# Hybrid Hyena and attention layer on one core: thirteen gate pairs by seven half-products, placed behind all branch projections

## The chip, the cores and the metric

The kernel runs on one core of a Trainium2 chip. The time is device microseconds for one launch; the span is the time from the first to the last instruction in the hardware profile of one such execution. Lower is better.

## The reference

One encoder layer: 512 tokens, width 2048, all in float32. Cut to what matters here:

```python
h = rms_norm(x, mix_norm_g)                       # (512, 2048)
proj = h @ w_in
u_h, q, k, v, g = jnp.split(proj, [c0, c1, c2, c3], axis=-1)   # g: 2 x 2048 columns
y_h = ...        # Hyena branch, (512, 1024), from u_h
y_a = ...        # attention branch, (512, 1024), from q, k, v
g_h, g_a = jnp.split(jax.nn.sigmoid(g + b_gate), 2, axis=-1)
merged = g_h * (y_h @ w_br_hyena) + g_a * (y_a @ w_br_attn)
x = x + merged @ w_out
h2 = rms_norm(x, ffn_norm_g)
return x + (jax.nn.silu(h2 @ w_ffn_gate) * (h2 @ w_ffn_up)) @ w_ffn_down   # inner width 5632
```

The merge, on which the change works, is the line of `merged` with the 2 x 2048 gate columns of `proj`: 16 blocks of 128 channels, and for each block one gate column block for Hyena, one for attention, and one branch projection of each.

## The kernel before

Activations lie with channels on the 128 partitions and the 512 tokens along the free axis. A matrix product takes 128 x 128 weight blocks as the stationary operand and a 128 x 512 activation tile as the moving one. For float32 accuracy each operand is split into a rounded high part and a remainder (`hi`, `lo`), and a block costs three matmuls (`mm3`): hi x hi, hi x lo, lo x hi.

Weights are packed by the host into tiles of eight blocks (512 KB) in the order of use (`weight_blocks`). `wblk` loads the next tile on SP's queue into one of two `raw` buffers, ScalarE casts the high part (three buffers), VectorE subtracts to get the remainder (three buffers). `group` runs one output block over its k blocks. `tmp` is a pool of five 128 x 512 scratch tiles that all stages share. PSUM has eight banks.

Instructions are written with tiles and the framework's scheduler orders them within each engine's queue; only TensorE's are kept in the order in which they are written. A queue runs in the order that the scheduler chose, and waits are on semaphores. The pools marked `reuse_waits="tile"` lie over older ones and wait tile by tile.

Stages, in TensorE's order:

1. Hyena projections, filters and convolutions; attention. Their results are `yh` and `ya`, eight tiles each, in pool `r3`. The normalised input `xg` stays split in pool `r1` (16 `hi`, 16 `lo`).
2. Merge. `gate_pair(m)` computes the two gate blocks of channel block m: two groups of 16 k blocks, 96 matmuls, then on VectorE a multiplication by the token scale `rbc` and on ScalarE a sigmoid. Three pairs (`GATES_AHEAD`) run ahead. Then, for each m, two branch groups of eight k blocks (48 matmuls), a multiplication of each by its gate, an addition into the merged row `mg`, and the gate pair m + 3. The branch inputs are split into a pool `r2` of their own.
3. The 16 merged rows, all in SBUF, are split into `r1` (`ms`), and 16 groups make the output projection `o`. `x2_tile` adds the residual, `x_sums` and `x_split` prepare what the FFN needs.
4. FFN gate and up. Two k halves, two columns blocks and two token halves make a 2 x 2 block product, done with seven products of halves in place of eight. `x_sums` builds the seven combinations of the activation for a pair of rows p (tile `V`, 128 x 7 x 256), `x_split` splits them (tile `X`; five pairs live in pool `xa`, three in `xb`, which lies over `r1`). For each group, VectorE builds four sums of weight tiles (`wsum`), ScalarE and VectorE split seven weight tiles (`wsplit`), `product` runs eight matmuls of 512 columns and eight of 256 for each of the seven, over PSUM banks `x` (two), `y` and `z`, and `fold` and half-width VectorE steps add the results up. The first group is written apart, since pairs 5 to 7 can be split only when `r1` is free, and takes in the norm of the new rows (`rs2`). 44 groups; `finish` closes each.
5. Down projection in three parts, most activations by way of DRAM (`actd`, `actr`), with the first four outputs side by side (`WIDE`).

The seven products, as the groups run them (`hl` is a split weight tile, `i` the combination of activations):

```python
for p in range(p0, p1):
    x = xs[p][:, i * 2 * H:(i + 1) * 2 * H]
    mm(bank, hi[:, p * P:(p + 1) * P], x, first and p == 0, False, skip_group_check=True)
for p in range(p0, p1):
    x = xs[p][:, i * 2 * H:(i * 2 + 1) * H]
    mm(bank[:, H:], lo[:, p * P:(p + 1) * P], x, False, p == NP - 1, skip_group_check=True)
```

Of the kernel before, what the change touches and what calls it, by code (L numbers as in the profile page):

```python
# [56 lines left out]
def weight_blocks():  # L57
# [25 lines left out]
    def quadrant(name, half, j):  # L83
        return [(name, k * P, j * P, P) for k in range(half, KT, 2)]

    for j in range(0, FT, 2):
        for name in ("w_ffn_gate", "w_ffn_up"):
            for half, c in ((0, 0), (0, 1), (1, 1), (1, 0)):
                out += quadrant(name, half, j + c)
# [11 lines left out]
def layer_kernel(tc, wpk, xT, par, flt, zemb, w4, decT, tbl, tb2, rope, qkg, out):  # L101
# [10 lines left out]

    def ps_tile(name):
        return psm.tile([P, S], F32, tag="ps", bufs=8, name=name)
# [622 lines left out]

    gts = [gate_pair(m) for m in range(GATES_AHEAD)]
# [3 lines left out]
    r2 = tc.alloc_tile_pool(name="r2", bufs=1)  # L742
    yhs = [split(r2, t, "hi2", "lo2", 16, 16, f"yhs{i}") for i, t in enumerate(yh)]
    yas = [split(r2, t, "hi2", "lo2", 16, 16, f"yas{i}") for i, t in enumerate(ya)]

    merged = []
    for m in range(KT):
        gs = gts[m]
        mg = r3.tile([P, S], F32, tag="r", bufs=16, name=f"mg{m}")
        for i, src in enumerate((yhs, yas)):  # L750
            bp = ps_tile(f"b{i}{m}")
            group(bp, src)
            nc.vector.tensor_tensor(gs[i] if i else mg, bp, gs[i], ALU.mult)
        nc.vector.tensor_tensor(mg, mg, gs[1], ALU.add)
        merged.append(mg)
        if m + GATES_AHEAD < KT:
            gts.append(gate_pair(m + GATES_AHEAD))
    ms = [split(r1, t, "hi", "lo", 16, 16, f"ms{i}") for i, t in enumerate(merged)]

    r2.release()
    r3.release()
    H = 256
    NP = KT // 2
    SQ = 7 * H
    pad = tc.alloc_tile_pool(name="pad", bufs=1, side="right")  # L770
# [6 lines left out]
    def ev(name):  # L777
        return wq.tile([P, H], F32, tag="ev", bufs=6, name=name)

    nffg = cpool.tile([P, P], F32, name="nffg")  # L780
    nc.vector.tensor_scalar(nffg[:, :KT], prm[:, PC["ffng"]:PC["ffng"] + KT], -1.0, None, ALU.mult)
    x2d = [dpool.tile([P, S], F32, tag=f"x2d{m}", bufs=1, name=f"x2d{m}") for m in range(KT)]
    actd = [dpool.tile([P, S], F32, tag=f"actd{j}", bufs=1, name=f"actd{j}") for j in range(FT)]
    acc2 = tmp("acc2")

    NRAW = 6
    raws = {"n": 0, "base": None}
    late = {}

    def raw_tile(i, name):  # L790
        n = raws["n"] % NRAW
        raws["n"] += 1
        if n < 2:
            t = wpool.tile([P, BLK * P], F32, tag="raw", bufs=2, name=name)
        elif n < NRAW - 1:
            t = wq.tile([P, BLK * P], F32, tag="rb", bufs=NRAW - 3, name=name)
        else:
            t = late["rc"].tile([P, BLK * P], F32, tag="rc", bufs=1, name=name)
        nc.sync.dma_start(t, wpk[i])
        return t  # L800

    def x2_tile(m, op):
        xt = tmp(f"x2{m}")
        nc.scalar.dma_start(xt, xT[m])
        nc.vector.tensor_tensor(xt, op, xt, ALU.add)
        nc.gpsimd.dma_start(x2d[m], xt)
        return xt

    xs = [None] * NP

    def x_sums(p, xe, xo):

        V = vp.tile([P, SQ], F32, tag="V", bufs=3, name=f"V{p}")
        b12 = ev(f"b12{p}")
        v = [V[:, i * H:(i + 1) * H] for i in range(7)]
        ge, go, ngo = pcol("ffng", 2 * p), pcol("ffng", 2 * p + 1), nffg[:, 2 * p + 1:2 * p + 2]
        nc.scalar.activation(v[0], xe[:, :H], AF.Copy, scale=ge)
        nc.scalar.activation(b12, xe[:, H:], AF.Copy, scale=ge)
        nc.vector.tensor_tensor(v[2], b12, v[0], ALU.subtract)
        nc.scalar.activation(v[1], xo[:, :H], AF.Copy, scale=go)  # L820
        nc.scalar.activation(v[5], xo[:, H:], AF.Copy, scale=ngo)
        nc.vector.scalar_tensor_tensor(v[4], v[5], -1.0, b12, ALU.mult, ALU.subtract)
        nc.vector.scalar_tensor_tensor(v[3], v[4], -1.0, v[0], ALU.mult, ALU.subtract)
        nc.vector.scalar_tensor_tensor(v[6], v[3], -1.0, v[1], ALU.mult, ALU.subtract)
        return V

    def x_split(p, V, cuts):
        pool = xa if p < NEARLY else late["xb"]
        X = pool.tile([P, 2 * SQ], F32R, tag="X", bufs=NEARLY if p < NEARLY else NP - NEARLY, name=f"X{p}")
        X4 = X.rearrange("p (i h t) -> p i h t", i=7, h=2)  # L830
        V3 = V.rearrange("p (i t) -> p i t", i=7)
        for a, b in zip(cuts, cuts[1:]):
            nc.scalar.copy(X4[:, a:b, 0, :], V3[:, a:b])
            nc.vector.tensor_tensor(X4[:, a:b, 1, :], V3[:, a:b], X4[:, a:b, 0, :].bitcast(F32), ALU.subtract)  # L834
        xs[p] = X

    def wsum(name, a, b):
        t = late["sg"].tile([P, BLK * P], F32, tag="sg", bufs=3, name=name)
        nc.vector.tensor_tensor(t, a, b, ALU.add)
        return t  # L840

    def wsplit(w, name, pool=wpool, bufs=3):
        hi = pool.tile([P, BLK * P], F32R, tag="whi", bufs=bufs, name=f"wh{name}")
        lo = pool.tile([P, BLK * P], F32R, tag="wlo", bufs=bufs, name=f"wl{name}")
        nc.scalar.copy(hi, w)  # L845
        nc.vector.tensor_tensor(lo, w, hi.bitcast(F32), ALU.subtract)  # L846
        return hi, lo

    def product(bank, hl, i, first, p0=0, p1=NP):
        hi, lo = hl  # L850
        for p in range(p0, p1):
            x = xs[p][:, i * 2 * H:(i + 1) * 2 * H]
            mm(bank, hi[:, p * P:(p + 1) * P], x, first and p == 0, False, skip_group_check=True)
        for p in range(p0, p1):
            x = xs[p][:, i * 2 * H:(i * 2 + 1) * H]
            mm(bank[:, H:], lo[:, p * P:(p + 1) * P], x, False, p == NP - 1, skip_group_check=True)

    def fold(name, b):
        t = ev(name)
        nc.scalar.copy(t, b[:, :H])  # L860
        nc.vector.tensor_tensor(t, b[:, H:], t, ALU.add)  # L861
        return t

    def group_raws(n):

        b = raws["base"] + 4 * n
        t = {}
        for q, name in ((0, "a11"), (3, "a12"), (1, "a21"), (2, "a22")) if n == 0 else \
                ((0, "a11"), (1, "a21"), (2, "a22"), (3, "a12")):
            t[name] = raw_tile(b + q, f"{name}_{n}")  # L870
        return t

    def bank(b, n):
        return psf.tile([P, S], F32, tag=b, bufs=2 if b == "x" else 1, name=f"f{b}{n}")

    xt = []
    V = {}
    for m in range(KT):
        if m == KT - 1:
            raws["base"] = state["tile"]  # L880
        op = ps_tile(f"o{m}")
        group(op, ms)
        xt.append(x2_tile(m, op))
        if m % 2:
            p = m // 2
            if p < NP - 1:
                V[p] = x_sums(p, xt[m - 1], xt[m])
            if p < NEARLY:
                x_split(p, V[p], (0, 7))
        if m < KT - 1:  # L890
            sumsq_add(acc2, xt[m], m, "x2sq")
    raws["base"] = state["tile"]
    psm.release()
    psf = tc.alloc_tile_pool(name="psf", bufs=1, space=PSUM, reuse_waits="tile")
    w0 = group_raws(0)
    h11 = wsplit(w0["a11"], "a11_0")
    x, y, z = (bank(b, 0) for b in "xyz")
    product(x, h11, 0, True, 0, NEARLY)
    h12 = wsplit(w0["a12"], "a12_0")
    product(z, h12, 1, True, 0, NEARLY)  # L900
    r1.release()
    late["sg"] = tc.alloc_tile_pool(name="sgp", bufs=1, reuse_waits="tile")
    late["xb"] = tc.alloc_tile_pool(name="xb", bufs=1, reuse_waits="tile")
    s1 = wsum("s1_0", w0["a21"], w0["a22"])
    hs1 = wsplit(s1, "s1_0")
    product(y, hs1, 2, True, 0, NEARLY)
    w4 = tc.alloc_tile_pool(name="w4", bufs=1, reuse_waits="tile")
    s2 = wsum("s2_0", s1, w0["a11"])
    hs2 = wsplit(s2, "s2_0", w4, 1)
    V[NP - 1] = x_sums(NP - 1, xt[-2], xt[-1])  # L910
# [48 lines left out]
    for n in range(FT):  # L959
# [24 lines left out]
        if n > 0:  # L984
            product(z, wsplit(w0["a12"], f"a12_{n}"), 1, True)
# [193 lines left out]
```

## Time and profile before

| | |
|---|---|
| median of 3 runs | 2646.08 us (2644.96 to 2646.10) |
| the profiled execution | 2646.29 us, span 2644.5 us |
| mean granted TensorE clock | 0.994 |
| TensorE matmul busy | 2610.4 us |
| VectorE, ScalarE busy | 1643.9 us, 1020.7 us |
| branches and gates interleaved | from 648.7 to 1105.7 us |
| output projection | from 1105.7 to 1279.7 us |
| FFN gate and up, 44 groups | from 1279.7 to 2155.8 us |

How to read it: a matmul's length in the profile is modelled and overlaps the next one's, so the length of a stage is taken from the starts of its pieces in the chain that ended last, not from busy time. Idle time of an engine counts only where the chain passes through it. In the tables by stretch, the columns are the stretch, its length, the busy time of TensorE, its weight load, VectorE, ScalarE and GpSimd with the number of instructions, the granted TensorE clock, the DMA engines' busy share, and GB/s. In a timeline, the brackets hold how long the engine sat idle before the instruction and what it waited for.

### The profile page before, as it was taken

How to read it: one execution, taken by the hardware profiler on the slowest of the kernel's cores; microseconds unless marked ns; L12 is line 12 of the kernel's file. 1: busy time of each engine (PE TensorE's matmuls, PEld its weight loads, DVE VectorE, ACT ScalarE, POOL GpSimd, SP SyncE). 2: the span in 40 equal slices, each digit the busy share in tenths (PEclk: the TensorE clock that was granted, in tenths of full speed). 3: DMA queues.
4: the chain of work that ended last, by engine and by line, in shares of the span. 5: the costliest groups of instructions: out<-in, count | busy, mean ns of one | idle time of the engine just before them, and what ended most of it. 6: DMA issues, size and time to landing. Idle time of an engine off the chain costs nothing.

```text
span 2644.5 us, 32721 instructions
## 1 busy us (share of the span) xinstructions
PE 2610.4 (99%) x12966; PEld 2208.5 (84%) x12966; DVE 1643.9 (62%) x2338; ACT 1020.7 (39%) x1482; POOL 86.5 (3%) x166
## 2 busy tenths in 40 slices
PE   9899999999999999999899999999999999999999
PEld 7788888888888888888788888888888888788887
DVE  7777763666333333544698989989889862443333
ACT  6443433566222222333444444444444442321111
POOL 1000001110000000000000000000000000000000
PEclk9999999999999999999899999999999999999999
DMA  6332333211223332344233333333333343442343
GB/s 223 104 100 89 110 109 105 70 57 64 96 96 97 100 98 96 131 143 145 98 110 112 123 128 125 115 120 128 120 121 120 119 149 102 150 146 96 128 144 107
DMA packets 93973, 303.63 MB, mean 115 GB/s; under 512 B 11227, under 2 KB 12251, under 8 KB 93820
## 3 DMA queue, kind: packets, MB, share of 16 engines
q1 hardware_dynamic: 71856, 251.69, 29.0%
q10 hardware_dynamic: 13068, 23.63, 3.0%
q0 software_dynamic: 8896, 26.22, 2.8%
q8 instruction: 101, 1.65, 0.3%
q14 instruction: 52, 0.43, 0.0%
HBM read 278.43 MB, written 23.07 MB: 114 GB/s over the span
## 4 chain that ended last, share of the span: by engine, by line
PE 94%; DVE 3%; DMA 1%; ACT 1%; issue 1%; ACTq 0%; DVEq 0%
PE fx L117 19%; PE d L117 18%; PE g L117 13%; PE fy L117 9%; PE o L117 7%; PE b L117 7%; PE px L117 6%; PE fz L117 5%; PE phv L117 3%; PE q L117 2%; PE kv L117 2%; PE up L117 1%; PE kp L117 1%; PE ab L117 1%; PE av L117 1%; PE sp L117 1%
## 5 line engine op out<-in xcount | busy, mean ns | idle before, releaser
L166 ACT CAST wh<-wr 128x1024 fp32r<-128x1024 f32 (+1 forms) x291 | 304.0, 1045 | 887.3 <-PE d L117 297.5
L167 DVE TENSOR_TENSOR wl<-wr,wh 128x1024 fp32r<-128x1024 f32 (+1 forms) x291 | 352.3, 1211 | 457.5 <-ACT wh L166 457.3
L117 PE MATMUL d<-act,wh 128*128 128x512 f32 x1408 | 435.6, 390 | 2.5 <-DVE act L935 1.7
L117 PEld LDWEIGHTS d<-act,wh 128*128 128x128 f32 x1408 | 264.2, 188 | 61.0 <-DVE act L935 3.8
L845 ACT CAST whs<-s 128x1024 fp32r<-128x1024 f32 x176 | 185.1, 1052 | 244.6 <-PE fx L117 113.1
L117 PE MATMUL d<-act,wl 128*128 128x512 f32 x704 | 273.9, 389 | 0.0
L846 DVE TENSOR_TENSOR wls<-s,whs 128x1024 fp32r<-128x1024 f32 x176 | 214.7, 1220 | 8.3 <-ACT whs L845 2.2
L845 ACT CAST wha<-a 128x1024 fp32r<-128x1024 f32 x132 | 138.8, 1052 | 205.8 <-PE fx L117 99.3
L117 PE MATMUL g<-xh,wh 128*128 128x512 f32 x512 | 200.4, 391 | 0.0
L117 PE MATMUL g<-xl,wh 128*128 128x512 f32 x512 | 199.3, 389 | 0.0
L117 PE MATMUL g<-xh,wl 128*128 128x512 f32 x512 | 199.3, 389 | 0.0
L117 PE MATMUL fx<-X,wha 128*128 128x512 f32 x704 | 179.1, 396 | 5.8 <-DVE X L834 3.0
L117 PE MATMUL fx<-X,whs 128*128 128x512 f32 x704 | 178.1, 395 | 0.4 <-DVE v L861 0.4
L117 PE MATMUL fy<-X,whs 128*128 128x512 f32 x704 | 177.2, 393 | 0.0
L846 DVE TENSOR_TENSOR wla<-a,wha 128x1024 fp32r<-128x1024 f32 x132 | 161.1, 1221 | 8.4 <-ACT wha L845 4.7
L117 PEld LDWEIGHTS d<-act,wl 128*128 128x128 f32 x704 | 132.2, 188 | 27.1
L117 PEld LDWEIGHTS fx<-X,wha 128*128 128x128 f32 x704 | 127.8, 191 | 29.5 <-issue 5.7
L117 PEld LDWEIGHTS fx<-X,whs 128*128 128x128 f32 x704 | 127.6, 190 | 23.9 <-DVE v L861 0.9
L117 PEld LDWEIGHTS fy<-X,whs 128*128 128x128 f32 x704 | 126.7, 189 | 22.9 <-DVE v L861 0.2
L117 PEld LDWEIGHTS g<-xh,wl 128*128 128x128 f32 x512 | 96.1, 188 | 20.1
L117 PEld LDWEIGHTS g<-xh,wh 128*128 128x128 f32 x512 | 96.2, 188 | 19.2
L117 PEld LDWEIGHTS g<-xl,wh 128*128 128x128 f32 x512 | 96.2, 188 | 19.1
(1203 smaller groups left out, 4788.3 us busy)
## 6 DMA issues: line engine op xcount, KB each, us to landing
wr<-wpk SPq DMA_DIRECT2D x287, 512.0 KB, 3.3
a<-wpk SPq DMA_DIRECT2D x176, 512.0 KB, 3.8
actd<-c POOLq DMA_DIRECT2D x40, 256.0 KB, 5.0
actr<-actd ACTq DMA_DIRECT2D x40, 256.0 KB, 3.8
xr<-xT SPq DMA_DIRECT2D x16, 256.0 KB, 6.0
K<-kd POOLq DMA_DIRECT2D x16, 256.0 KB, 3.0
x<-xT ACTq DMA_DIRECT2D x16, 256.0 KB, 2.9
x2d<-x POOLq DMA_DIRECT2D x16, 256.0 KB, 3.3
```

The costliest lines, as they stand in the source:

```text
L117: tc.keep_in_program_order(nc.tensor.matmul(out, lhsT=lhsT, rhs=rhs, start=start, stop=stop, **kw))
L166: nc.scalar.copy(hi[:, c], raw[:, c])
L167: nc.vector.tensor_tensor(lo[:, c], raw[:, c], hi[:, c].bitcast(F32), ALU.subtract)
L845: nc.scalar.copy(hi, w)
L846: nc.vector.tensor_tensor(lo, w, hi.bitcast(F32), ALU.subtract)
```

## The change

- Gate pairs 0 to 2 stay as they were. The other thirteen run as seven-product groups of the FFN's form, on the input scaled by `mix_norm_g` and `rbc`, after all 16 branch pairs. Their weights are packed in the FFN's quarter order.
- The code of the seven products becomes a function `seven` with `x_sums`, `x_split` and `run`, used for the gates ("g") and the FFN ("f").
- The branch inputs are split into the `hi` and `lo` tiles of `r1`, in place of the normalised input; `r2` is gone. For m of 0 to 2 the branch result is multiplied by its gate and the merged row written to DRAM (`md`). For m from 3 on, ScalarE copies each branch result out of PSUM and POOL's queue writes it to DRAM (`bd`).
- Beside branch pairs 3 to 10, the input rows are loaded again, multiplied by `rbc`, and made into `V` and `X` (pairs 0 to 4).
- `gate_finish` closes a gate group: sigmoid, load of the branch result on ScalarE's queue, multiplication, addition, write of the merged row to `md`.
- The output projection loads all 16 rows from `md`, splits them, and runs its first four outputs side by side; what follows an output (`o_rest`) is as before.
- The negated gains (`ngain`) are made for both norms, earlier.

Cut to its core:

```diff
     for m in range(KT):
         out += cols("w_br_hyena", m * P, HT) + cols("w_br_attn", m * P, HT)
-        if m + GATES_AHEAD < KT:
-            out += gates(m + GATES_AHEAD)
-    for m in range(KT):
+    for m in range(GATES_AHEAD, KT):
+        quarters("w_in", C_GH + m * P, C_GA + m * P)
+    for k in range(KT):
+        out += [("w_out", k * P, m * P, P) for m in range(WIDE)]
+    for m in range(WIDE, KT):
         out += cols("w_out", m * P, KT)
...
-    r2 = tc.alloc_tile_pool(name="r2", bufs=1)
-    yhs = [split(r2, t, "hi2", "lo2", 16, 16, f"yhs{i}") for i, t in enumerate(yh)]
+    yhs = [split(r1, t, "hi", "lo", 16, 16, f"yhs{i}") for i, t in enumerate(yh)]
...
+    def x_rows(k):
+        t = tmp(f"xg{k}")
+        nc.scalar.dma_start(t, xT[k])
+        nc.vector.tensor_tensor(t, t, rbc, ALU.mult)
         return t
...
+    for m in range(KT):
+        for i, src in enumerate((yhs, yas)):
+            bp = ps_tile(f"b{i}{m}")
+            group(bp, src)
+            if m < GATES_AHEAD:
+                nc.vector.tensor_tensor(gts[m][i], bp, gts[m][i], ALU.mult)
+            else:
+                t = tmp(f"bt{i}{m}")
+                nc.scalar.copy(t, bp)
+                nc.gpsimd.dma_start(bd[i][m], t)
+        if m < GATES_AHEAD:
+            nc.vector.tensor_tensor(gts[m][0], gts[m][0], gts[m][1], ALU.add)
+            nc.gpsimd.dma_start(md[m], gts[m][0])
+        elif m >= GATES_AHEAD and m - GATES_AHEAD < NP:
+            p = m - GATES_AHEAD
+            V[p] = x_sums(p, x_rows(2 * p), x_rows(2 * p + 1))
+            if p < NEARLY:
+                x_split(p, V[p], (0, 7))
+
+    def gate_finish(n, c):
+        m = n + GATES_AHEAD
+        for i, t in enumerate(c):
+            nc.scalar.activation(t, t, AF.Sigmoid, bias=pcol("bgate", i * KT + m))
+            b = tmp(f"br{i}{m}")
+            nc.scalar.dma_start(b, bd[i][m])
+            nc.vector.tensor_tensor(t, t, b, ALU.mult)
+        nc.vector.tensor_tensor(c[0], c[0], c[1], ALU.add)
+        nc.gpsimd.dma_start(md[m], c[0])
...
+    run(KT - GATES_AHEAD, r1, c_gates, gate_finish)
...
+    for m in range(KT):
+        t = tmp(f"mg{m}")
+        nc.scalar.dma_start(t, md[m])
+        hl = r1.tile([P, 2 * S], F32R, tag="ms", bufs=KT, name=f"ms{m}")
+        nc.scalar.copy(hl[:, :S], t)
+        nc.vector.tensor_tensor(hl[:, S:], t, hl[:, :S].bitcast(F32), ALU.subtract)
+        ms.append((hl[:, :S], hl[:, S:]))
...
+    ops = [ps_tile(f"o{m}") for m in range(WIDE)]
+    for k in range(KT):
+        for op in ops:
+            wh, wl = wblk()
+            mm3(op, wh, wl, ms[k][0], ms[k][1], k == 0, k == KT - 1)
```

More of the change, by code (lines that the diff above doesn't have):

```diff
@@ L111, in layer_kernel @@
     psm = tc.alloc_tile_pool(name="psm", bufs=1, space=PSUM)
+    banks = {"pool": psm, "n": 8}
     def ps_tile(name):
-        return psm.tile([P, S], F32, tag="ps", bufs=8, name=name)
+        return banks["pool"].tile([P, S], F32, tag="ps", bufs=banks["n"], name=name)
     def mm(out, lhsT, rhs, start, stop, **kw):
@@ L736, in gate_pair @@
         return gs
+    H = 256
+    NP = KT // 2
+    SQ = 7 * H
+    NRAW = 6
+    ngain = cpool.tile([P, P], F32, name="ngain")
+    for i, name in enumerate(("ffng", "mixg")):
+        nc.vector.tensor_scalar(ngain[:, i * KT:(i + 1) * KT], prm[:, PC[name]:PC[name] + KT], -1.0, None, ALU.mult)
+    bd = [[dpool.tile([P, S], F32, tag=f"bd{i}{m}", bufs=1, name=f"bd{i}{m}") for m in range(KT)] for i in range(2)]
+    md = [dpool.tile([P, S], F32, tag=f"md{m}", bufs=1, name=f"md{m}") for m in range(KT)]
@@ L741, in layer_kernel @@
     at.release()
-    r2 = tc.alloc_tile_pool(name="r2", bufs=1)
-    yhs = [split(r2, t, "hi2", "lo2", 16, 16, f"yhs{i}") for i, t in enumerate(yh)]
[L744 to L765, printed above, removed]
+    yhs = [split(r1, t, "hi", "lo", 16, 16, f"yhs{i}") for i, t in enumerate(yh)]
+    yas = [split(r1, t, "hi", "lo", 16, 16, f"yas{i}") for i, t in enumerate(ya)]
     r3.release()
[L767 to L770, printed above, removed]
+    pad = tc.alloc_tile_pool(name="pad", bufs=1, side="right", reuse_waits="tile")
     pad_t = pad.tile([P, 112], F32, name="pad_t")
@@ L775, in layer_kernel @@
     vp = tc.alloc_tile_pool(name="vp", bufs=1, side="right", reuse_waits="tile")
[L777 to L799, printed above, removed]
-        return t
@@ L802, in x2_tile @@
[L802 to L874, printed above, removed]
-    xt = []
[L877 to L883, printed above, removed]
+    x_sums, x_split, V, run = seven("g", 1)
@@ new lines, in gate_finish, with c_gates @@
+    def gate_finish(n, c):
[7 more added lines that the diff above has]
+        nc.gpsimd.dma_start(md[m], c[0])
+    def c_gates(n, cp):
+        return [cp.tile([P, S], F32, tag="c", bufs=4, name=f"gc{i}_{n}") for i in range(2)]
@@ new lines, in layer_kernel @@
+    run(KT - GATES_AHEAD, r1, c_gates, gate_finish)
+    banks["pool"].release()
+    pso = tc.alloc_tile_pool(name="pso", bufs=1, space=PSUM, reuse_waits="tile")
+    banks.update(pool=pso, n=8)
+    r1 = tc.alloc_tile_pool(name="r1o", bufs=1, reuse_waits="tile")
+    ms = []
+    for m in range(KT):
[5 more added lines that the diff above has]
+        ms.append((hl[:, :S], hl[:, S:]))
@@ L884, in layer_kernel, with o_rest @@
+    vp = tc.alloc_tile_pool(name="vpf", bufs=1, side="right", reuse_waits="tile")
+    x_sums, x_split, V, run = seven("f", 0)
+    xt = []
+    acc2 = None
+    def o_rest(m, op):
+        t = tmp(f"x2{m}")
+        nc.scalar.dma_start(t, xT[m])
+        nc.vector.tensor_tensor(t, op, t, ALU.add)
+        nc.gpsimd.dma_start(x2d[m], t)
+        xt.append(t)
         if m % 2:
@@ L890, in layer_kernel @@
         if m < KT - 1:
[L891 to L910, printed above, removed]
-    for p in range(NEARLY, NP):
-        x_split(p, V[p], (0, 3, 7))
-        product(x, h11, 0, True, p, p + 1)
-        product(z, h12, 1, True, p, p + 1)
-        product(y, hs1, 2, True, p, p + 1)
-    sumsq_add(acc2, xt[-1], KT - 1, "x2sq")
-    v1, v5 = fold("v1_0", x), fold("v5_0", y)
-    product(x, hs2, 3, False)
-    w4.release()
-    vp.release()
-    late["rc"] = tc.alloc_tile_pool(name="rcp", bufs=1, reuse_waits="tile")
-    cp = tc.alloc_tile_pool(name="cp", bufs=1, reuse_waits="tile")
-    ea = tc.alloc_tile_pool(name="ea", bufs=1, side="right", reuse_waits="tile")
+            sumsq_add(acc2, t, m, "x2sq")
+    ops = [ps_tile(f"o{m}") for m in range(WIDE)]
[3 more added lines that the diff above has]
+            mm3(op, wh, wl, ms[k][0], ms[k][1], k == 0, k == KT - 1)
+    acc2 = tmp("acc2")
+    for m in range(KT):
+        if m < WIDE:
+            op = ops[m]
+        else:
+            op = ps_tile(f"o{m}")
+            group(op, ms)
+        o_rest(m, op)
     rbc2 = cpool.tile([P, S], F32, tag="bc", bufs=1, name="rbc2")
-    acts = {}
+    acts, gated = {}, {}
     def act_tile(j, pool, bufs):
@@ L935, in act_split, with early_pool, c_ffn, swiglu @@
         nc.vector.tensor_tensor(lo, src, hi.bitcast(F32), ALU.subtract)
-    gated = {}
-    ps_tile_main = ps_tile
-    def ps_tile(name):
-        return psf.tile([P, S], F32, tag="ps", bufs=3, name=name)
-    def finish(n, c):
+    def early_pool():
+        nonlocal ea
+        ea = tc.alloc_tile_pool(name="ea", bufs=1, side="right", reuse_waits="tile")
+    def c_ffn(n, cp):
+        return [tmp(f"c{i}_{n}") if n % 2 else cp.tile([P, S], F32, tag="c", bufs=4, name=f"c{i}_{n}")
+                for i in range(2)]
+    def swiglu(n, c):
         j, up = n // 2 * 2, n % 2
@@ L996, in layer_kernel @@
-    state["tile"] = raws["base"] + 4 * FT
-    state["pos"] = BLK
-    for p in (cp, late["rc"], late["xb"], late["sg"]):
-        p.release()
-    psf.release()
+    ea = None
+    run(FT, r1, c_ffn, swiglu, sums=lambda: x_sums(NP - 1, xt[-2], xt[-1]), side_pool=early_pool,
+        norm=lambda: sumsq_add(acc2, xt[-1], KT - 1, "x2sq"))
+    banks["pool"].release()
     psd = tc.alloc_tile_pool(name="psd", bufs=1, space=PSUM, reuse_waits="tile")
-    def ps_tile(name):
-        return psd.tile([P, S], F32, tag="ps", bufs=8, name=name)
+    banks.update(pool=psd, n=8)
```

196 lines of the change are left out of this document (155 added, 41 removed).

## The prediction

> **What bounds the kernel now.** I read the page first (shares and the chain that ended last), then that chain in order of time, which gives each stage's length, then tables by stretch at the stage borders, and then each engine's timeline around those borders.
>
> ```profile
> span 2644.5 us, 32721 instructions
> PE 2610.4 (99%) x12966; PEld 2208.5 (84%) x12966; DVE 1643.9 (62%) x2338; ACT 1020.7 (39%) x1482; POOL 86.5 (3%) x166
> PE 94%; DVE 3%; DMA 1%; ACT 1%; issue 1%; ACTq 0%; DVEq 0%
> ```
>
> TensorE is the bound: 94% of the chain. A change pays if it removes matmul time without opening a gap in which TensorE waits. The chain in order of time:
>
> ```profile
> 648.69 10.88 PE b L117 x48
> 659.57 21.76 PE g L117 x96
> ...
> 1051.25 21.76 PE g L117 x96
> 1073.01 32.64 PE b L117 x144
> 1105.65 174.09 PE o L117 x768
> ...
> 1297.92 0.80 PE rs2ss L117 x8
> ...
> 1313.43 1.28 PE rs2bcp L117 x8
> ```
>
> Branch pairs (b, 48 matmuls, 10.88 us) and gate pairs (g, 96 matmuls, 21.76 us) alternate without a piece between them; 13 gate pairs lie between 659.57 and 1073.01. The output projection (o) follows at once. The first seven-product group of the FFN does not run smoothly, as a table by stretch shows (us, busy time of each engine, granted TensorE clock, DMA share, GB/s):
>
> ```profile
> 1279.74:1289.00 9.26, 6.55 (x36) 5.17 (x36) 9.23 (x12) 6.75 (x9) 0.54 (x1) 1.00 0.08 30
> 1289.00:1298.00 9.00, 8.35 (x31) 6.71 (x32) 6.98 (x9) 3.52 (x6) 0.00 (x0) 0.62 0.17 59
> ...
> 1314.71:1334.27 19.56, 19.56 (x114) 17.21 (x113) 17.61 (x23) 10.93 (x14) 0.00 (x0) 1.00 0.31 108
> 1314.70:2155.80 841.10, 841.08 (x4818) 740.00 (x4817) 750.25 (x990) 391.91 (x521) 21.05 (x39) 1.00 0.36 119
> ```
>
> Groups 2 to 44 take 841.1 / 43 = 19.56 us each with TensorE never idle. The first takes 1314.71 - 1279.74 = 34.97 us, 15.4 more, with waits and a stretch of 9 us in which the clock is 0.62.
>
> **The change part by part.**
>
> *Thirteen gate pairs become seven-product groups.* Removed: 13 x 21.76 = 282.9 us of TensorE. Added: 13 groups of the form that the FFN runs, 13 x 19.56 = 254.3. Gain 28.6 us, if they run as the FFN's do. Would they? The FFN's group has VectorE busy 750.25 / 43 = 17.45 us of 19.56. The gates' end swaps two multiplications for two and an addition. Rows that bear on it, of the groups (busy, mean ns, idle before and its releaser), the DMA issues (us to landing) and VectorE's timeline:
>
> ```profile
> L753 DVE TENSOR_TENSOR gt<-b,gt 128x512 f32<-128x512 f32 x16 | 11.1, 692 | 46.8 <-PE b L117 46.8
> L734 ACT ACTIVATE gt<-gt,prm 128x512 f32<-128x512 f32 x32 | 23.2, 724 | 11.1 <-DVE gt L733 11.1
> ...
> L1027 DVE TENSOR_TENSOR dacc<-dacc,x2r 128x512 f32<-128x512 f32 x16 | 11.0, 688 | 1.6 <-DMA x2r<-x2d 1.6
> ```
> ```profile
> actr<-actd ACTq DMA_DIRECT2D x40, 256.0 KB, 3.8
> ```
> ```profile
> 2137.03 0.41 DVE L994 TENSOR_TENSOR c<-d,fx 128x256 f32<-128x256 f32 x1
> 2137.36 1.22 DVE L846 TENSOR_TENSOR wls<-s,whs 128x1024 fp32r<-128x1024 f32 x1
> 2138.49 0.68 DVE L948 TENSOR_TENSOR c<-c,rbc 128x512 f32<-128x512 f32 x1
> ```
>
> One operation more, 0.69 us: 18.1 of 19.56, 93%. ScalarE: 391.91 / 43 = 9.1 us, plus two sigmoids of 0.72 for one activation: about 10. Both fit. New in a group are two loads of branch results (256 KB, 3.8 us to land as the reloads of `actr` do) that a VectorE multiplication waits for, with the next group's weight sums and splits behind it in VectorE's queue and TensorE behind those. The loads depend only on a free scratch tile of five, so they can go out early. The queue is also not in written order: a split of the next group (L846) stands between a group's last step (L994) and its first closing multiplication (L948), and the existing addition of a reloaded tile (L1027) waited 1.6 us over 16 times. Price 0, hidden by the 1.5 us of slack; the other end is the second rival.
>
> *The branches move together.* The rows, of two stretches (branches alone, output projection), of groups, and of ScalarE's timeline:
>
> ```profile
> 1073.00:1105.70 32.70, 32.70 (x146) 27.07 (x145) 14.19 (x18) 8.35 (x10) 0.00 (x0) 1.00 0.34 106
> ```
> ```profile
> 1105.65:1279.74 174.09, 174.09 (x770) 144.15 (x769) 80.01 (x98) 63.99 (x85) 8.14 (x15) 1.00 0.47 145
> ```
> ```profile
> L166 ACT CAST wh<-wr 128x1024 fp32r<-128x1024 f32 (+1 forms) x291 | 304.0, 1045 | 887.3 <-PE d L117 297.5
> L167 DVE TENSOR_TENSOR wl<-wr,wh 128x1024 fp32r<-128x1024 f32 (+1 forms) x291 | 352.3, 1211 | 457.5 <-ACT wh L166 457.3
> ...
> L834 DVE TENSOR_TENSOR X<-V,X 128x1792 fp32r<-128x1792 f32 (+2 forms) x11 | 16.4, 1513 | 9.1 <-ACT X L833 9.1
> L833 ACT CAST X<-V 128x1792 fp32r<-128x1792 f32 (+2 forms) x11 | 13.9, 1282 | 11.0 <-DVE V L824 9.8 <-PE o L117 1.2
> L1031 ACT COPY dacc<-d 128x512 f32<-128x512 f32 x16 | 9.4, 585 | 16.1 <-PE d L117 15.9
> ```
> ```profile
> 1280.49 0.51 ACT L820 ACTIVATE V<-x,prm 128x256 f32<-128x256 f32 x1 [2.34 <-DVE x L805]
> ```
>
> 16 x 10.88 us stay. From the fourth on each also carries, in 10.88 us: VectorE two weight remainders (1.21), two input multiplications (0.69), four sums of half width (0.41), a split of 1.51: 7.0 us; ScalarE two casts (1.05), two copies out of PSUM (0.59), four scalings (0.51), a cast of 1.28: 6.6 us. Four 256 KB transfers per pair (two writes on POOL's queue, two loads on ScalarE's) add 1.05 MB / 10.88 us = 96 GB/s. Branches alone run at 106 GB/s; about 200 is more than the 145 of the o stage, where TensorE never waits. Price 0, cover: 4 us of slack per pair on both engines and two raw weight buffers. Up to 3 us if a late weight load shows once. SP issues the same weight tiles in another order. POOL, 3% busy, issues 42 writes more (26 branch results, 16 merged rows) at 0.54 us each (its column in the first stretch above); nothing on TensorE's path waits for them within 20 us but the last merged row.
>
> *The branch splits take the tiles of the normalised input.* They can't run before the third gate pair's second half has used each tile (10.88 us long, 0.68 per tile); a split step is at most 0.69 us (VectorE at this width), so they follow TensorE and the first is ready long before it is read. Price 0, bound 2 us.
>
> *Branches to gates, a new border.* The nearest row is the o-to-FFN border, 15.4 us, and 0 is the other end (the group's matmuls are fixed, so nothing below). What made the 15.4:
>
> ```profile
> 1279.77 0.69 DVE L805 TENSOR_TENSOR x<-o,x 128x512 f32<-128x512 f32 x1 [3.36 <-PE o L117]
> 1280.38 1.22 DVE L839 TENSOR_TENSOR s<-a,a 128x1024 f32<-128x1024 f32 x1
> 1287.93 4.09 DVE L834 TENSOR_TENSOR X<-V,X 128x768 fp32r<-128x768 f32 x4
> 1289.03 0.47 PE L117 MATMUL fx<-X,wha 128*128 128x512 f32 x1 [2.32 <-DVE X L834]
> 1290.94 0.80 PE L117 MATMUL fx<-X,wha 128*128 128x512 f32 x1 [0.63 <-DVE X L834]
> 1307.97 3.75 PE L117 MATMUL fx<-X,wha 128*128 128x512 f32 x8 [2.89 <-DVE c L983]
> ```
>
> VectorE's queue stood 3.36 us before the last residual addition (L805), and the weight sums and X splits were queued behind it; so TensorE waited 2.32 and 0.63 us for X. Its last wait, 2.89, is for the reading of bank x (L983), behind norm work and weight splits. The clock dip came after the waits. In the gates' border there is no residual addition, V is complete five pairs earlier, and there is no norm (rs2 matmuls 0.80 + 1.28, and its small VectorE steps). VectorE's chain starts some 4 us earlier (3.36 + 0.69) and lacks three sums of 0.41: 5.3 us against the 2.95 that TensorE waited. The X waits go; late next is the bank's reading, for no z product stands between in a first group: 1.2 (three steps of 0.4) to 2.9 us. With part of a clock dip I take 4 us, nearer 0 than 15.4, since two of three causes are absent.
>
> [...] Here waits of 2.32 and 0.63 us already go before a 0.62 clock. [...]
>
> *Gates to output projection, a new border.* Before, merged rows stayed in SBUF; now 16 are loaded (ScalarE's queue), split, and stand where the group's scratch was. The nearest rows, FFN to down projection:
>
> ```profile
> 2149.83 1.40 ACTq L1014 DMA_DIRECT2D actr<-actd  x3
> 2155.63 0.63 PE L117 MATMUL d<-act,wh 128*128 128x512 f32 x2
> 2157.16 1.05 ACT L166 CAST wh<-wr 128x1024 fp32r<-128x1024 f32 x1 [3.74 <-DMA wr<-wpk]
> 2158.38 0.61 ACT L934 CAST act<-actr 128x512 fp32r<-128x512 f32 x1
> 2160.44 2.66 DVE L935 TENSOR_TENSOR act<-actr,act 128x512 fp32r<-128x512 f32 x4
> ```
>
> There TensorE went straight on, on four activations kept in SBUF. The loads had been issued, but the first split of a loaded one began 2.75 us after the switch and its remainder 4.8 after it, behind a cast that waited 3.74 us for weights. The gates keep nothing, so TensorE would stand until the first merged row is split. Ends: 0 (the first three rows lie over weight sums that are free before the last product) and 8 (4.8 us idle, then a dip like 9 us at 0.62, 3.4 us lost). I take 4. Behind it the supply holds: with four outputs at once a row feeds 12 matmuls, 2.72 us, while splits take 0.7. The last row's chain (two half-width steps, sigmoid, multiplication, addition, then a write and a load at 3.8 us each: some 11 us) has 15 x 2.72 = 41 us. Its load stands in ScalarE's queue until the write has landed, with weight casts behind it; the three cast buffers hold 3 x 5.44 us of work.
>
> *Output projection to FFN.* Same steps; the X tiles now lie over rows that the last product frees a little earlier. Price 0, between -3 and +2.
>
> **Sum.** The profiled execution took 2646.29 us (span 2644.5), 0.2 over the median 2646.08. 2646.3 - 28.6 + 4 + 4 = 2625.7; I say 2626.
>
> **The rivals.**
> - *Both borders dear*: 15.4 and 8 us: 2646.3 - 28.6 + 23.4 = 2641. For it: the measured first group. Against: its two causes that are absent. 0.20.
> - *Slower: VectorE's queue stands at the new multiplications.* If sigmoid, load and multiplication were queued as written, VectorE would stand for a sigmoid and a load, 0.72 + 3.8 = 4.5 us per group, with the next group's splits behind it; less 1.5 of slack, 3 us x 13 = 39: 2646.3 - 28.6 + 8 + 39 = 2665. It decides from a gate group of 19.56 + 20.6 / 13 = 21.1 us on. Against it: the two rows named above, of a queue that isn't in written order and of reloads that came in time. 0.09.
> - *The gain is eaten within the groups*: at 21.1 us each, where the second rival begins: about 2646. 0.04.
> - *Borders free*: next to nothing at both, and -3 at the FFN's: 2615 and below. 0.05.
>
> **How the numbers follow.** The forecast case (2615 to 2636) has 0.62. No change is within 0.2%, 5.3 us, about what can be told. Faster: 0.62 + 0.05 + 0.13 of the dear borders (2641 lies at the bound) = 0.80; same: 0.07 + 0.04 = 0.11; slower 0.09. The range 2613 to 2642 leaves out the slow cases and a little below.
>
> **What would show it.** Right: g matmuls of three pairs only, thirteen groups of 19.56 us at full clock, one border before them of 20 to 26 us, o's first matmul up to 5 us after the last product, branches at 10.88. Wrong: gate groups over 19.6 with VectorE waiting on a branch load; a clock under 1.00 at both new borders; TensorE waiting on weights among the branches.

## The result, and the profile after

The changed kernel takes 2628.6 us (median; 2626.91 to 2630.14), the kernel before beside it 2645.77: a ratio of 0.9936, 95% interval 0.9924 to 0.9947. Run again with the later experiments it took 2629.28 against 2644.8, ratio 0.9945 (0.9931 to 0.9958). The forecast was 2626, the range 2613 to 2642. The profiled execution took 2628.62 us, its span 2626.8: 17.7 us under the span before.

The page of the changed kernel, its shares and its chain; then that chain in order of time:

```profile
span 2626.8 us, 33854 instructions
PE 2583.3 (98%) x13174; PEld 2198.8 (84%) x13174; DVE 1811.7 (69%) x2593; ACT 1115.0 (42%) x1642; POOL 109.2 (4%) x208
PE 93%; DVE 4%; DMA 1%; ACT 1%; issue 1%; ACTq 0%; DVEq 0%
```
```profile
629.77 19.75 PE g L121 x87
649.52 174.09 PE b L121 x768
829.26 5.14 DVE gX L790 x5
...
846.31 5.86 PE gx L121 x32
...
1088.97 176.64 PE o L121 x768
1273.88 4.01 DVE fX L790 x4
...
1292.00 4.35 PE fx L121 x16
```

TensorE is still the bound. In this part of the kernel VectorE stands in the chain at the first group of both seven-product stages, with the splits of X longest; before, it did so at the FFN's only. By stretch (us; busy time of PE, PEld, DVE, ACT, POOL; granted clock, DMA share, GB/s): branches, first gate group, the other twelve, the FFN's first group.

```profile
649.50:823.60 174.10, 174.10 (x770) 144.25 (x769) 81.96 (x99) 68.51 (x96) 15.17 (x28) 1.00 0.46 157
823.60:849.40 25.80, 20.85 (x113) 17.21 (x113) 25.55 (x30) 15.17 (x19) 0.54 (x1) 1.00 0.52 173
849.40:1084.00 234.60, 234.60 (x1344) 206.36 (x1343) 211.29 (x286) 115.44 (x157) 6.49 (x12) 1.00 0.42 148
...
1265.60:1297.20 31.60, 24.21 (x130) 19.93 (x129) 28.93 (x46) 16.23 (x22) 0.54 (x1) 0.95 0.25 92
```

Twelve groups take 234.6 / 12 = 19.55 us each at full clock, TensorE never idle. The first takes 25.8 and the FFN's first 31.6. What TensorE waited for at the three borders (its timeline; the wait and its releaser in brackets):

```profile
831.32 0.50 PE L121 MATMUL gx<-gX,gwha 128*128 128x512 f32 x1 [1.23 <-DVE gX L790]
833.32 0.50 PE L121 MATMUL gx<-gX,gwha 128*128 128x512 f32 x1 [0.69 <-DVE gX L790]
835.93 2.09 PE L121 MATMUL gx<-gX,gwhs 128*128 128x512 f32 x8 [1.28 <-DVE gv L837]
846.31 2.11 PE L121 MATMUL gx<-gX,gwha 128*128 128x512 f32 x8 [1.75 <-DVE gc L907]
1088.97 1.52 PE L121 MATMUL o<-ms,wh 128*128 128x512 f32 x2 [4.97 <-ACT ms L995]
1274.89 0.47 PE L121 MATMUL fx<-fX,fwha 128*128 128x512 f32 x1 [2.31 <-DVE fX L790]
1276.81 0.51 PE L121 MATMUL fx<-fX,fwha 128*128 128x512 f32 x1 [0.63 <-DVE fX L790]
1292.00 3.40 PE L121 MATMUL fx<-fX,fwha 128*128 128x512 f32 x8 [2.87 <-DVE c L907]
```

The account, spans against spans: 13 x (21.76 - 19.56) = -28.6; first gate group 25.8 for 19.56, +6.2; before the projection 4.97 us of standing, and its matmuls in 176.64 for 174.09 us, +7.5; the FFN's first group 31.6 for 35.0, -3.4; branches begin at 649.5 for 648.7, +0.8. Sum -17.5, measured -17.7.

### The profile page after: what moved, and what is told of

The parts are those of the page before. It is cut to its first block, busy times and chain, and to the rows that moved or that the text cites. A ratio compares the mean times of both kernels' runs of the same rounds, so it can differ in the third digit from the quotient of the medians.

```text
span 2626.8 us, 33854 instructions
## 1 busy us (share of the span) xinstructions
PE 2583.3 (98%) x13174; PEld 2198.8 (84%) x13174; DVE 1811.7 (69%) x2593; ACT 1115.0 (42%) x1642; POOL 109.2 (4%) x208
## 4 chain that ended last, share of the span: by engine, by line
PE 93%; DVE 4%; DMA 1%; ACT 1%; issue 1%; ACTq 0%; DVEq 0%
PE fx L121 19%; PE d L121 18%; PE fy L121 9%; PE o L121 7%; PE b L121 7%; PE px L121 6%; PE gx L121 5%; PE fz L121 5%; PE phv L121 3%; PE gy L121 3%; PE q L121 2%; PE g L121 2%; PE kv L121 2%; PE gz L121 1%; PE up L121 1%; PE kp L121 1%
## 5 line engine op out<-in xcount | busy, mean ns | idle before, releaser
L821 ACT CAST fwhs<-fs 128x1024 fp32r<-128x1024 f32 x176 | 185.1, 1052 | 244.0 <-PE fx L121 112.8
L821 ACT CAST fwha<-fa 128x1024 fp32r<-128x1024 f32 x132 | 138.7, 1052 | 205.2 <-PE fx L121 96.2
L822 DVE TENSOR_TENSOR fwls<-fs,fwhs 128x1024 fp32r<-128x1024 f32 x176 | 214.7, 1220 | 8.4 <-ACT fwhs L821 2.2
L121 PE MATMUL fx<-fX,fwha 128*128 128x512 f32 x704 | 178.5, 395 | 5.8 <-DVE fX L790 2.9
L121 PE MATMUL fx<-fX,fwhs 128*128 128x512 f32 x704 | 176.6, 393 | 1.2 <-DVE fv L837 1.2
L121 PE MATMUL fy<-fX,fwhs 128*128 128x512 f32 x704 | 177.0, 393 | 0.0
L822 DVE TENSOR_TENSOR fwla<-fa,fwha 128x1024 fp32r<-128x1024 f32 x132 | 161.1, 1221 | 8.8 <-ACT fwha L821 5.4
L121 PE MATMUL o<-ms,wh 128*128 128x512 f32 x512 | 159.7, 393 | 5.0 <-ACT ms L995 5.0
L121 PEld LDWEIGHTS d<-act,wl 128*128 128x128 f32 x704 | 132.5, 188 | 27.2
L121 PEld LDWEIGHTS fx<-fX,fwha 128*128 128x128 f32 x704 | 127.8, 191 | 29.4 <-issue 5.7
L121 PEld LDWEIGHTS fx<-fX,fwhs 128*128 128x128 f32 x704 | 126.7, 189 | 24.2 <-DVE fv L837 1.7
```

The costliest lines, as they stand in the source:

```text
L121: tc.keep_in_program_order(nc.tensor.matmul(out, lhsT=lhsT, rhs=rhs, start=start, stop=stop, **kw))
```

## Experiments

Ratios are to the kernel before, run beside each. Lengths "from the branches on" go from the first branch matmul to the end of the output projection: 616.1 us in the changed kernel (1088.97 + 176.64 - 649.52).

**Place and detour alone.** The kernel before, with this part of the change only (cut, comments added; the branch results are written as in the change):

```diff
+    for m in range(GATES_AHEAD, KT):
+        gs = gate_pair(m)                      # 8 products, 21.76 us
+        mg = r3.tile([P, S], F32, tag="r", bufs=16, name=f"mg{m}")
+        for i in range(2):
+            b = tmp(f"br{i}{m}")
+            nc.scalar.dma_start(b, bd[i][m])   # branch result by way of DRAM
+            nc.vector.tensor_tensor(gs[i] if i else mg, b, gs[i], ALU.mult)
```

> The kernel before with one part of the change: all branch projections run first, 13 pairs of branch results go to DRAM and come back, and the gate pairs behind them stay eight-product ones (21.76 us each); merged rows stay in SBUF. Theory (placement and detour are hidden beside TensorE, the gain is that of the seven products alone): 2646, between 2643 and 2650, with every gate pair at 21.76 us. Rival (the detour has a price of its own that the seven products overcame): 1 us or more for each of 13 pairs, 2658 or above.

2644.16 us, ratio 1.0001 (0.9991 to 1.0011). Its stretches:

```profile
650.35:824.43 174.08, 174.08 (x770) 144.14 (x769) 45.76 (x42) 46.48 (x59) 13.54 (x25) 1.00 0.39 136
824.43:1107.15 282.72, 282.72 (x1250) 234.08 (x1248) 113.16 (x126) 78.57 (x93) 0.54 (x1) 1.00 0.38 125
```

The 13 gate pairs stand in one piece of 282.7 us, 21.75 each, with no wait. Placement and detour cost nothing. The change's gain and loss lie in what this kernel leaves out, above all the seven products, their borders, and the merged rows' way through DRAM (here they stay in SBUF).

**How much room VectorE has.** Two or four more VectorE operations per gate group, ahead of its sigmoids:

```diff
+        for t in c:
+            for _ in range(1):   # 2 in the other kernel
+                nc.vector.tensor_tensor(t, t, t, ALU.max)
```

> The changed kernel with two more VectorE operations of 128x512 in each gate group (1.24 us; four took 2.49 and lengthened most groups by 1.41 to 1.67 us, to 21.0 or 21.2). Theory A (VectorE has some 1.1 us per group that it can give, the rest of its idle time lies where the next product isn't there yet): groups of 19.6 to 19.8 us, 2628 to 2631. Theory B (all idle time counts, 1.95 us, and the four operations cost more by their place in the queue): no group longer than 19.56, 2628. Rival (a cost in proportion, half of that of four): groups of 20.2 us, 2637.

> The changed kernel with four more VectorE operations of 128x512 (maximum of a tile with itself, no change of values) in each gate group, ahead of its sigmoids: some 2.4 to 2.8 us more work for VectorE in a group of 19.55 us in which it is busy 17.6. Theory (VectorE's queue is full only when its work exceeds the group): groups of 20.0 to 20.4 us, 12 or 13 times 0.45 to 0.85, 2634 to 2640. Rival (VectorE's order leaves no slack, every operation shows): groups of 22 to 22.4 us, 2660 or above, and so the forecast's slower rival was near.

Two more: 2630.68 us in one run, the twelve groups at 19.55 us. Four more: 2647.19 us, ratio 1.0012 (1.0002 to 1.0021). The stretch of twelve groups with two more; of ten groups with four more, and a wait there:

```profile
850.30:1084.90 234.60, 234.60 (x1345) 206.34 (x1344) 225.69 (x310) 115.41 (x155) 6.49 (x12) 1.00 0.43 149
```
```profile
865.70:1074.39 208.69, 198.20 (x1121) 172.19 (x1121) 202.66 (x281) 97.97 (x130) 5.40 (x10) 1.00 0.40 137
```
```profile
878.28 2.11 PE L121 MATMUL gy<-gX,gwhs 128*128 128x512 f32 x8 [1.41 <-ACT gwhs L821]
```

With VectorE busy 225.69 / 12 = 18.8 of 19.55 us nothing is lost within the groups (theory B; A's groups of 19.6 to 19.8 us did not show). What that run lost lies at the borders: TensorE waited 5.82 us before the projection in place of 4.97, and the clock fell in the first gate group. At 202.66 / 10 = 20.27 us of work a group takes 20.87, VectorE's work and 0.6 us in which it idles, and TensorE waits for ScalarE's cast of a weight sum that VectorE finished late; I had expected 20.0 to 20.4. So the groups become VectorE's somewhere between 18.8 and 20.3 us of its work. The changed kernel, at 211.29 / 12 = 17.6, is at least 1.2 us below that point.

**Branches to gates.** Two edits: the last pair's branches in the other order (their weights are packed in that order too); with it, the copies of the last pair's results on VectorE instead of ScalarE.

```diff
-        for i, src in enumerate((yhs, yas)):
+        for i, src in ((1, yas), (0, yhs)) if m == KT - 1 else ((0, yhs), (1, yas)):
```
```diff
-                nc.scalar.copy(t, bp)
+                if m == KT - 1:
+                    nc.vector.tensor_copy(t, bp)
+                else:
+                    nc.scalar.copy(t, bp)
```

> The changed kernel with the last pair's two branch projections in the other order, so that the tiles in which the first gate group's weight sums lie are read for the last time 5.4 us earlier. Theory (VectorE's chain for the first gate group waits for the last branch matmul because those sums lie over its input): the sums start 3.3 us earlier or more, the waits of 1.23 and 0.69 us for X go, the first group takes 23.5 to 24 instead of 25.8 us, 2626.5. Rival (ScalarE's X cast is queued behind the copy of the last branch result, or the reads of the banks set the end): the first group keeps 25.8 us, 2628.6.

> The changed kernel with the last pair's two branches swapped, and with the last two branch results copied out of PSUM by VectorE instead of ScalarE. Theory (ScalarE's casts of X stood behind the copy that waits for the last branch): the casts begin 2 us earlier or more, the waits of 1.23 and 0.69 us go, the first gate group without slow clock takes about 24 us. Rival (the casts wait for TensorE themselves, since X lies over a tile of the last branch's input): they begin where they did, 0.5 us after the last branch, and the waits stay at 1.2 and 0.7.

2629.2 us, ratio 0.9944 (0.9929 to 0.9959), and 2630.66 us in one run: no gain. In the changed kernel (VectorE's timeline, then ScalarE's) the first weight sum waits for the last branch matmul, and so do ScalarE's copy and, behind it, the casts of X:

```profile
823.64 1.22 DVE L815 TENSOR_TENSOR gs<-ga,ga 128x1024 f32<-128x1024 f32 x1 [3.35 <-PE b L121]
```
```profile
823.63 0.59 ACT L958 COPY bt<-b 128x512 f32<-128x512 f32 x1 [4.13 <-PE b L121]
824.12 1.78 ACT L789 CAST gX<-gV 128x768 fp32r<-128x768 f32 x2
```

With the branches swapped, the second sum ran at 819.93, ahead of the last branch's end at 821.9, but VectorE then stood for the cast, and TensorE waited as before:

```profile
819.93 1.23 DVE L817 TENSOR_TENSOR gs<-gs,ga 128x1024 f32<-128x1024 f32 x1
823.47 0.96 DVE L792 TENSOR_TENSOR gX<-gV,gX 128x768 fp32r<-128x768 f32 x1 [2.31 <-ACT gX L791]
```
```profile
829.78 0.50 PE L123 MATMUL gx<-gX,gwha 128*128 128x512 f32 x1 [1.23 <-DVE gX L792]
```

With ScalarE freed of the copy too, the cast itself waits for the last branch:

```profile
823.05 2.52 ACT L791 CAST gX<-gV 128x768 fp32r<-128x768 f32 x3 [4.61 <-PE b L123]
```

So it isn't queue order: the tiles of X lie over the input of the last branch, whichever of the two that is (in the built program each of the three late tiles of X lies over inputs of both). That the border would shrink with memory for X of its own wasn't tried.

**Gates to output projection.** First, the splits of rows 0 to 2 in tiles that are free long before (of tag `rb`). Then the same with four unused PSUM tiles allocated ahead of the outputs, meant to move these to other banks. Then the same rows, with the first four outputs in a pool of their own, banks 4 to 7 (cut; the other outputs then share the other four banks). And by itself, the loads issued on another queue.

```diff
-        hl = r1.tile([P, 2 * S], F32R, tag="ms", bufs=KT, name=f"ms{m}")
+        if m < NRAW - 3:
+            hl = wq.tile([P, 2 * S], F32R, tag="rb", bufs=NRAW - 3, name=f"ms{m}")
+        else:
+            hl = r1.tile([P, 2 * S], F32R, tag="ms", bufs=KT - NRAW + 3, name=f"ms{m}")
```
```diff
+    for i in range(4):
+        ps_tile(f"od{i}")
```
```diff
+    psw = tc.alloc_tile_pool(name="psw", bufs=1, space=PSUM, reuse_waits="tile")
...
-    ops = [ps_tile(f"o{m}") for m in range(WIDE)]
+    ops = [psw.tile([P, S], F32, tag="pw", bufs=WIDE, name=f"o{m}") for m in range(WIDE)]
```
```diff
-        nc.scalar.dma_start(t, md[m])
+        nc.gpsimd.dma_start(t, md[m])
```

> The changed kernel with the splits of the first three merged rows in tiles of their own, free long before the gates end, so that their casts stand earlier in ScalarE's queue. Theory (TensorE stood 4.97 us before the output projection because the first row's cast was queued behind the last sigmoid and a load that waits for a scratch tile, with the row itself loaded some 17 us before): the wait goes to under 0.5 us, the output projection's stage runs at full clock in 174.1 instead of 176.6 us, 2628.6 - 7.5 = 2621. Rival 1 (the rest of the row's chain or the weights arrive as late): the wait stays at 4 to 5 us, 2628. Rival 2 (the clock drop at the projection's start does not come from the wait): the wait goes, the stage stays at 176.6, 2624.

> The changed kernel with the first three merged rows in tiles of their own, and with the four output banks of the projection's start moved from the four banks of the gate products to the four others. Theory (with the rows split early, what TensorE waited for, 2.48 us, was the reading of the last product's bank, behind a weight cast and a remainder): the wait falls under 0.7 us, no slow clock follows, the output projection takes 174.1 to 174.5 us, and the time is 6 to 7.5 us under the changed kernel's, 2622. Rival (something else is late by the same 2 us, rows or weights): a wait of 2 us or more stays, 2626.

> The changed kernel with the first three merged rows in tiles of their own and the projection's four first outputs in a PSUM pool of their own, so that they lie in banks 4 to 7 and the last gate product (bank 0) is not under the first of them. Theory (with the rows early, TensorE waited 2.48 us for the reading of the last product's bank, because the program had laid the first output in that bank, also where the edit before this one meant to move it): the wait falls under 0.5 us, no slow clock at the projection's start, its 768 matmuls take 174.1 to 174.5 us from the last gate product on, 6 to 8 us under the changed kernel's 2628.6 to 2629.3: 2622. Rival (rows 1 and 2, cast behind the last weight casts, come late in place of the bank): waits of 1 to 2 us within the first 6 us of the projection, 2625.

> The changed kernel with the loads of the merged rows issued from POOL's queue instead of ScalarE's, everything else the same. Theory (the first row's cast stands in ScalarE's queue behind the gates' last sigmoid and behind a load that waits for a scratch tile): without the load the cast starts about 1.1 us earlier, TensorE's wait before the projection is 3.9 us instead of 4.97. Rival (the wait is that of the row's own load and its write before it): the wait stays at 5 us or grows, since POOL's queue issues the writes too.

In the changed kernel, ScalarE's timeline: the first load of a merged row, then the rows before the projection:

```profile
1050.01 0.33 ACTq L993 DMA_DIRECT2D mg<-md  x1
...
1086.46 0.72 ACT L973 ACTIVATE gc<-gc,prm 128x512 f32<-128x512 f32 x1 [1.34 <-DVE gc L918]
1087.94 0.33 ACTq L993 DMA_DIRECT2D mg<-md  x1
1088.30 1.14 ACT L995 CAST ms<-mg 128x512 fp32r<-128x512 f32 x2 [1.12 <-DVE gc L976]
```

The first row's cast stood behind the gates' last sigmoid and behind the issue of a load (1087.94) that waited for the multiplication of L976 to free a scratch tile; the row itself had been there for some 34 us (its load went out at 1050.01, and these loads took at most 4.1 us; the 17 us of the expectation were those of the rows after it). With the loads on POOL's queue, the cast follows the sigmoid and the wait is 3.74 us instead of 4.97, as expected (2629.17 us in one run; TensorE then stood another 0.75 us for the row's remainder). With the rows apart, the first cast was done at 1079.6, and TensorE waited for something else (one row of that kernel; the same wait with the unused tiles):

```profile
1088.17 0.73 PE L121 MATMUL o<-ms,wh 128*128 128x512 f32 x2 [2.48 <-DVE gc L918]
```
```profile
1088.53 0.73 PE L121 MATMUL o<-ms,wh 128*128 128x512 f32 x2 [2.48 <-DVE gc L918]
```

2627.09 us, 0.9935 (0.992 to 0.995), and 2626.06 us, 0.9928 (0.9915 to 0.994). My first theory fell by half: behind the late row stood the reading of the last product's bank (L918), queued behind a weight remainder. The unused tiles moved nothing: in the built program the first output still lay in bank 0, that of the last product. With a pool of its own:

```profile
1086.16 1.12 PE L121 MATMUL gx<-gX,gwla 128*128 128x256 f32 x8
1087.12 0.63 PE L121 MATMUL o<-ms,wh 128*128 128x512 f32 x2
```
```profile
1087.28 174.41 PE o L121 x768
```

No wait, full clock. From the branches on 1087.28 + 174.41 - 650.59 = 611.1 us, 5.0 less than in the changed kernel. The 7.5 us at the border are gone, but in this execution the clock fell to half in the first gate group, where the changed kernel's profile has it full. It is the lowest time of all, 2624.1 us, ratio 0.9926 (0.9912 to 0.9939), though by the times alone it can't be told from the changed kernel: the intervals overlap.

**The clock.** The changed kernel once more:

> The changed kernel once more, as the measure for the runs beside it, and as a test of the reading of the clock: in all profiles so far the clock is granted for stretches of 3.41 us on a grid that lies elsewhere in each run, and every stretch in which TensorE stood for 1.90 us or more (1.77 at most elsewhere) was followed by one or more at half speed. Theory (the grid's place decides): waits on TensorE at both borders as before (1.23, 0.69, 1.28, 1.75; 4.97; 2.31, 0.63, 0.75, 0.42, 2.87), but slow stretches may fall elsewhere, span 2625 to 2629. Rival (the same waits always give the same slow stretches): none in the first gate group, two at the output projection, one in the FFN's first group.

Its waits were the same (1.59 in place of 1.75 once), and so were its half-clock stretches: two at the projection, one in the FFN's first group. The grid lay only 0.2 us from the first profile's, so this run could not tell the two apart. The other kernels do. At the branches-to-gates border the changed kernel and the one with rows apart run the same instructions with the same waits for X; by stretches of 3.41 us (PE busy, clock, DMA share, GB/s), first the changed kernel, then the other:

```profile
827.20:830.61 3.41, 2.89 (x16) 1.00 0.90 285
830.61:834.03 3.42, 2.02 (x10) 1.00 0.06 24
834.03:837.44 3.41, 2.13 (x11) 1.00 0.47 132
```
```profile
829.85:833.26 3.41, 1.51 (x9) 1.00 0.19 67
833.26:836.68 3.42, 3.11 (x8) 0.50 0.04 13
836.68:840.09 3.41, 3.41 (x11) 0.50 0.95 342
```

One grid splits the two waits over two stretches, the other holds both in one, and the clock is at half for the next two. The same at the FFN's first group, before the change and after it:

```profile
1286.81:1290.22 3.41, 1.19 (x6) 1.00 0.00 0
1290.22:1293.64 3.42, 2.79 (x9) 0.50 0.00 0
1293.64:1297.05 3.41, 3.41 (x11) 0.50 0.20 54
```
```profile
1270.93:1274.35 3.42, 1.65 (x11) 1.00 0.00 0
1274.35:1277.76 3.41, 2.24 (x11) 1.00 0.00 0
1288.00:1291.41 3.41, 1.13 (x9) 1.00 0.48 178
1291.41:1294.83 3.42, 2.83 (x7) 0.50 0.02 5
```

So the FFN's first group became 3.4 us shorter although its long waits stayed (2.32, 0.63, 2.89 before; 2.31, 0.63, 2.87 after, and one more of 0.75): it had four stretches at half clock before and one after. In these rows the grid's place decides: at the first border a stretch with 1.51 us of matmuls went before half clock, and the same waits spread over two with 2.02 and 2.13 did not; at the FFN's border it was 1.19 us against 1.65 and 2.24. That the change has no part in that place, they don't show. In all ten kept profiles of kernels with seven-product gates this group took 31.6 to 31.9 us, in the two with eight-product gates 35.0 and, with place and detour alone, 33.6.

The first gate group went the other way. Its clock was full only in the changed kernel's two profiles. In the eight other kernels with seven-product gates one or two stretches there were at half clock, and the group took 27.2 to 28.3 us in place of 25.8; in seven of the eight the clock fell at the projection too.

## Why the prediction was right, step by step

- *Thirteen groups*: right. 19.55 us measured for 19.56. VectorE is busy 17.6 us per group where 18.1 was forecast, and the loads of branch results cost nothing, as said; the room left was shown with two more operations.
- *Branches together*: right, 174.1 us at full clock, 157 GB/s where "about 200" was estimated.
- *Branch splits in the input's tiles*: right, the gates' last matmul ends at 629.77 + 19.75 = 649.52, where the branches begin.
- *Branches to gates*: 4 forecast, 6.2 measured, and the reason failed. "VectorE's chain starts some 4 us earlier" and "the X waits go" were wrong: X waits of 1.23 and 0.69 us stayed, since sums and X lie over the last branch's input and must wait for its last matmul. A residual addition was absent, as said; memory took its place. The banks' readings (1.28 and 1.75) were inside the 1.2 to 2.9 named. The clock stayed full here, in both profiles of this kernel; the part of a clock dip that the term held showed in the eight other kernels, at 1.4 to 2.5 us.
- *Gates to projection*: 4 forecast, 7.5 measured. The wait was 4.97 us, at the end of "up to 5"; its price of 8, that of the nearest row, was the better one. The term was mis-sized because the tiles were thought free early enough: the casts stood in ScalarE's queue all the same, and the bank's reading behind them, 2.48 us, was not in the term.
- *Projection to FFN*: 0 forecast, -3.4 measured, outside its -3 to +2. The long waits stayed, as said; that fewer stretches at half clock follow them was not foreseen, and why stays open.
- *The sum*: the two new borders were 5.7 us dearer than forecast and the work ahead of them 0.8, the FFN's border 3.4 cheaper: 2625.7 + 3.1 = 2628.8. Part of the hit is luck, then, errors that cancel: with the FFN's border as before it would have been about 2632, between the forecast and the rival of two dear borders (2641).
- *Waits and the clock*: the forecast's reading, that waits of 2.32 and 0.63 us go before a slower clock, held in some kernels only. With no gap over 1.23 us the clock went to 0.50 (first gate group, rows apart: 1.22 and 0.68 us of standing in one stretch), and with the same waits it stayed at 1.00 (changed kernel: 1.23 and 0.69 us, in two stretches). Each stretch of 3.41 us shown above is wholly at 0.50 or at 1.00.
- *The rivals*: VectorE's queue did not stand at the new multiplications; its decisive point, 21.1 us per group, was not reached on the mean even with four more operations (20.87). The two new borders cost 6.2 + 7.5 = 13.7 us, between the 8 forecast and the 23.4 of the rival in which both are dear.

## What to carry to other kernels

Price a border by what memory and PSUM banks the new stage takes from the old one's last inputs, not by which dependencies are absent: the casts of X, the first output's bank and a reload's scratch tile all waited here for a place, not for data. When a wait is taken away, look for the one behind it: the late row hid a late bank. Compare border costs over several profiles, since the same waits (1.2 and 0.7 us) were followed by half clock in one kernel here and by full clock in another.

## What the runs showed of the hardware

In the profiles the clock stood at 1.00 or at 0.50 for whole stretches of 3.41 us, on a grid that lay elsewhere from run to run: in the changed kernel it fell at 1086.61 and at 1291.41, 60 stretches apart, and with rows apart at 833.26, between two edges of that grid (830.61 and 834.03). TensorE standing for 1.90 us or more of a stretch at full clock was followed by one or two at 0.50 (three, at the wait of 7.56 us before the projection in the kernel with four more operations). At 0.50 eight matmuls of 128x512 took 3.78 us, at 1.00 they took 2.00 (rows apart, from 835.85 and from 840.67). By an estimate from 0.50 and 3.41, each such stretch costs some 1.7 us if it is full of matmuls. In the twelve kept profiles, from 490 to 1340 us of the span, every stretch at full clock with up to 1.51 us of matmuls (rows apart, from 829.85) was followed by half clock, and none with 1.83 us or more (the lowest of them: the changed kernel once more, from 844.09). In between no sharp bound showed, with four stretches that kept the clock and five that lost it: in the kernel with two more operations it stayed after 1.54, and in the one with unused tiles it fell after 1.79:

```profile
1273.54:1276.95 3.41, 1.54 (x10) 1.00 0.00 0
1276.95:1280.37 3.42, 2.36 (x12) 1.00 0.01 2
```
```profile
829.92:833.34 3.42, 1.79 (x9) 1.00 0.16 58
833.34:836.75 3.41, 2.72 (x9) 0.50 0.32 62
```

What else counts there stays open.
